# The first modulation share: half of its sums on TensorE, between the transposes of x

## The chip, the cores and the metric

The kernel runs on one core of a Trainium2 chip. The metric is the device time of one launch in microseconds (us). The engines are TensorE (PE; PEld is its weight load), VectorE (DVE), ScalarE (ACT), GpSimd (POOL) and SyncE (SP), which here only issues transfers.

## The reference, cut to what matters

One transformer block over 512 tokens of 1024 features, all in fp32. What the change touches is the very start, where a condition vector `c` is turned into a shift and a scale for every feature and these are applied to the normalized input:

```
cond = jax.nn.silu(c)
mod = (cond @ ada_w[l] + ada_b[l]).reshape(B, 6, D_MODEL)[:, :, None, :]
shift1, scale1, gate1 = mod[:, 0], mod[:, 1], mod[:, 2]
u = rmsnorm(x, norm_mix[l]) * (1.0 + scale1) + shift1
aq, ak, av, bq, bkv, biq, bik, biw, cq, ck, cv, g = split_cols(u @ w_in[l])
```

Everything behind it (three attention branches, gates, output projection, a feed-forward layer and a last norm) is left as it is.

## The kernel before, in words

Every product of the block needs `u`, and `u` needs two things: the normalized x with features on partitions (`xnT`), and the shift and the scale of each feature (`ab`).

**x.** Four tiles of 128 tokens by 1024 features (512 KB each) are fetched into `xt`. For tile t, ACT squares and sums it (`x_square`, L317) and takes the root (L320), DVE takes the reciprocal (L321) and multiplies the tile by it (L322), TensorE turns it in eight 128x128 transposes into two PSUM tiles `xtp` (`x_turn`, L328), and `x_copy` (L336 on DVE, L338 on ACT) copies the two halves into `xnT`. The loop at L409 runs these steps of several tiles interleaved.

**The modulation shares.** shift1 and scale1 are `cond @ ada_w` over 1024 rows. The 1024 features are cut into four shares of 256 features. For share q, `fetch_share(q)` fetches eight row blocks k of 128 rows (256 KB each: 256 columns of the shift and 256 of the scale) into `ada`, and then three 256 KB slices of the first weights (`raw_b` twice, `raw_bq`). `mod_sums` multiplies every row block by its column of `cond` and adds up the blocks in two accumulators `gsum`: the first two blocks as a scaled copy on ACT (L356), the other six as multiply-and-add on DVE (L358), then the two accumulators are added (L360). What is left, a sum over the 128 partitions, is done by TensorE in `mod_columns` (L368): for each 128 features one matmul of the `gsum` block (as weights) with a column of ones, four of them in a share. DVE then adds the bias and makes `ab` (L371, L373), ACT makes `uh` (L377) out of `xnT` and `ab`, and TensorE's real work starts with `p_kv` (L448). From there the products of share q run while ACT and DVE make the sums of share q+1.

**The bias table.** Two small matmuls `tps` (L431) and two ACT copies `ts` (L432) make a table that the attention reads much later. They stand behind the loop over x.

**What sets the order.** The schedule is written out by hand: each engine runs its instructions in the order of the program text and waits in place. SP issues the transfers in program order as well. `warm(n)` (L457) issues n matmuls of the identity that nobody reads, 7 ahead of `mod_columns(0)` and 5 behind it.

Of the kernel before, what the change touches and what calls it, by code (L numbers as in the profile page):

```python
# [13 lines left out]
F32 = mybir.dt.float32  # L14
F32R = mybir.dt.float32r
AF = mybir.ActivationFunctionType
# [4 lines left out]
S = 512  # L21
D = 1024
NT = 4
KT = 8
# [95 lines left out]
def block_kernel(ctx: ExitStack, tc: tile.TileContext, x, c, rel_bias, ada_w, ada_b, norm_mix, w_in,  # L120
                 gate_b, diff_lambda, diff_subln, dsa_kv_norm, dsa_w_uv, w_br_a, w_br_b, w_br_c, w_o,
                 norm_mlp, w_ff1, w_ff2, norm_final, onehot, out):
    nc = tc.nc
    x, out = x[0], out[0]
# [9 lines left out]
    dram = ctx.enter_context(tc.tile_pool(name="dram", bufs=1, space=bass.MemoryType.DRAM))  # L134
# [5 lines left out]
    def bank(tag, name):  # L140
        return ps.tile([128, 512], F32, tag=tag, name=name, bufs=banks[tag])

    def big_tile(name, dt=F32, shape=(128, 8, 512)):
        return big.tile(list(shape), dt, tag="big", name=name)
# [8 lines left out]
    def rows(w, r0, nk, c0, n):  # L153
        return w[r0:r0 + nk * 128, c0:c0 + n].rearrange("(k p) c -> p k c", p=128)
# [105 lines left out]
    rb = const.tile([33, 12], F32, name="rb")  # L260
# [8 lines left out]
    start = ExitStack()  # L269
    st = start.enter_context(tc.tile_pool(name="st", bufs=1))  # L270
    oh = st.tile([33, 640], F32, name="oh")
    nc.gpsimd.dma_start(oh, onehot)
    xt = big_tile("xt", shape=(128, 4, 1024))
    for t in range(NT):
        nc.sync.dma_start(xt[:, t], x[t * 128:(t + 1) * 128])
    for r0, src, n in small_rows:
        nc.gpsimd.dma_start(vrow[r0:r0 + n], src.rearrange("o (r p) -> (o r) p", p=128))

# [2 lines left out]
    SHARES = ((0, 2), (2, 4), (4, 6), (6, 8))  # L281
    ada = {}
    for n in QS:
        pool, tag = (st, "") if n == "b1" else (wp, "raw")
        raws[n] = pool.tile([128, 8, 256], F32, tag=tag or "raw1", name=f"raw_{n}")

    def fetch_share(q):
        k0, k1 = SHARES[q]
        n, c0 = (k1 - k0) * 128, k0 * 128
        ada[q] = st.tile([128, 8, 2, 256], F32, tag="ada", name=f"ada{q}", bufs=2)[:, :, :, 0:n]  # L290
        if n == 128:
            for g in range(2):
                for sl in range(2):
                    nc.sync.dma_start(ada[q][:, 4 * g:4 * g + 4, sl, :], rows(ada_w, g * 512, 4, sl * 1024 + c0, n))
        else:
            for k in range(KT):
                nc.sync.dma_start(ada[q][:, k], ada_w[k * 128:(k + 1) * 128, 0:2048].rearrange(
                    "p (s c) -> p s c", s=2)[:, :, c0:c0 + n])
        for name in QS:
            nc.sync.dma_start(raws[name][:, k0:k1], chunks[name][0][:, k0:k1])  # L300

    for q in range(2):
        fetch_share(q)
# [3 lines left out]
    cond = const.tile([128, 8], F32, name="cond")  # L307
# [8 lines left out]
    def x_square(t):  # L316
        nc.scalar.activation(junk, xt[:, t], AF.Square, accum_out=xss[t])  # L317

    def x_norm(t):
        nc.scalar.activation(xss[t], xss[t], AF.Sqrt, bias=eps, scale=1.0 / D)  # L320
        nc.vector.reciprocal(xss[t], xss[t])  # L321
        nc.vector.tensor_scalar(xt[:, t], xt[:, t], xss[t], None, op0=ALU.mult)  # L322

    def x_turn(t):
        for g in range(2):
            tp = xtp[t, g] = bank(("S", "O")[g], f"xtp{t}{g}")
            for k in range(4):
                nc.tensor.transpose(tp[:, k * 128:(k + 1) * 128],  # L328
                                    xt[:, t, (4 * g + k) * 128:(4 * g + k + 1) * 128], ident)

    def x_copy(t):
        for g in range(2):
            dst = xnT[:, 4 * g:4 * g + 4, t * 128:(t + 1) * 128]
            srcv = xtp[t, g].rearrange("p (k q) -> p k q", k=4)
            if g == 0 and t < 2:
                nc.vector.tensor_copy(dst, srcv)  # L336
            else:
                nc.scalar.activation(dst, srcv, AF.Copy)  # L338
# [8 lines left out]
    def mod_sums(q, ks):  # L347

        n = 128 * (SHARES[q][1] - SHARES[q][0])
        if 0 in ks:  # L350
            gsum[q] = [st.tile([128, 2, 256], F32, tag=f"gsum{i}", name=f"gsum{q}{i}", bufs=2)[:, :, 0:n]
                       for i in range(2)]
        for k in ks:
            acc, src = gsum[q][k % 2], ada[q][:, k]
            if k < 2:
                nc.scalar.activation(acc, src, AF.Copy, scale=cond[:, k:k + 1])  # L356
            else:
                nc.vector.scalar_tensor_tensor(acc, src, cond[:, k:k + 1], acc, op0=ALU.mult, op1=ALU.add)  # L358
        if KT - 1 in ks:
            nc.vector.tensor_tensor(gsum[q][0], gsum[q][0], gsum[q][1], op=ALU.add)  # L360

    def mod_columns(q):
        k0, k1 = SHARES[q]
        nk = k1 - k0
        gps = bank("S", f"gps{q}")
        for s in range(2):
            for k in range(nk):
                nc.tensor.matmul(gps[:, s * nk + k:s * nk + k + 1], gsum[q][0][:, s, k * 128:(k + 1) * 128], ones,  # L368
                                 start=True, stop=True)
        ks = slice(k0, k1)  # L370
        nc.vector.tensor_tensor(ab[:, :, ks], gps[:, 0:2 * nk].rearrange("p (s k) -> p s k", s=2), vmod[:, :, ks],  # L371
                                op=ALU.add)
        nc.vector.scalar_tensor_tensor(ab[:, 1, ks], ab[:, 1, ks], 1.0, vcol[:, C_NM + k0:C_NM + k1],  # L373
                                       op0=ALU.add, op1=ALU.mult)
# [31 lines left out]
    nc.vector.tensor_scalar(cond, cond, 1.0, None, op0=ALU.add)  # L406
    nc.vector.reciprocal(cond, cond)
    nc.vector.tensor_tensor(cond, cond, cps[:, 0:8], op=ALU.mult)
    for t in range(NT + 2):  # L409
        if t < NT:  # L410
            x_square(t)
            x_norm(t)
        if t == NT - 1:
            mod_sums(0, (0, 1))
        if t > 1:
            x_copy(t - 2)
        if t == NT:
            vps = bank("T", "vps")
            nc.tensor.transpose(vps[:, 0:C_ALL], vrow, ident[0:C_ALL, 0:C_ALL])
            nc.scalar.activation(vcol, vps[:, 0:C_ALL], AF.Copy)  # L420
        if 0 < t <= NT:
            x_turn(t - 1)
    mod_sums(0, range(2, KT))


    tab = dram.tile([12, 640], F32, name="tab")
    tabw = [dram.tile([4, 128, 640], F32, name=f"tabw{g}") for g in range(3)]
    ts = st.tile([12, 640], F32, name="ts")
    for a, b, tag in ((0, 512, "S"), (512, 640, "T")):
        tps = bank(tag, f"tps{a}")  # L430
        nc.tensor.matmul(tps[0:12, 0:b - a], rb, oh[:, a:b], start=True, stop=True)  # L431
        nc.scalar.activation(ts[:, a:b], tps[0:12, 0:b - a], AF.Copy)  # L432
    nc.gpsimd.dma_start(tab, ts)

    first = {n: bank(tag, f"p_{n}") for n, tag in (("kv", "mm"), ("iq0", "mm"), ("iq1", "S"), ("ik", "S"),
                                                   ("bq00", "O"), ("bq01", "O"))}

# [16 lines left out]
    def warm(n):  # L454

        for _ in range(n):
            nc.tensor.matmul(warm_ps[:, 0:128], ident, ident, start=True, stop=True)  # L457

    LAST = len(SHARES) - 1
    warm(7)  # L460
    mod_columns(0)
    warm(5)
    split_share(0, QS[:1])
    make_uh(0)
    split_share(0, QS[1:])
    make_ul(0)
    mod_sums(1, range(4))

    def first_two(q):
# [3 lines left out]
    for q in range(LAST):  # L473
        if q + 2 <= LAST:
            fetch_share(q + 2)
        mod_sums(q + 1, range(4, KT))
        rest = b_part(2, q)
        for _ in chain(first_two(q), islice(rest, 4)):
            pass
        split_share(q + 1, QS[:1])  # L480
        if q + 2 <= LAST:
            mod_sums(q + 2, (0, 1))
        mod_columns(q + 1)
        make_uh(q + 1)
        if q + 2 <= LAST:
            mod_sums(q + 2, (2, 3))
        split_share(q + 1, QS[1:])
        make_ul(q + 1)
        if q + 1 == LAST:
            fetch(3)  # L490
            fetch(4)
        for _ in rest:
            pass
# [706 lines left out]
    tns, tps = {}, {}  # L1200
# [381 lines left out]
```

## Time and profile before

| | |
|---|---|
| three runs | 844.58, 839.05, 843.79 us, median 843.79 us |
| the profiled execution | 841.24 us, its span (first to last instruction) 839.5 us |
| mean granted clock of TensorE in it | 0.995 |
| TensorE busy | 808.7 us (96%) |
| VectorE busy | 570.8 us (68%) |
| ScalarE busy | 411.7 us (49%) |
| moved by DMA | 116.48 MB, mean 139 GB/s |

The page of the profile gives busy time by engine and the span in 40 slices; TensorE is at 0.8 or more in every slice but the first (0.5) and the last (0.6). So the program is one long row of TensorE work, and its start is the only stretch where TensorE has little to do for long. The timeline lists an engine's instructions in order, neighbours of one kind merged: start, duration until the last of them ends, engine, line, operation, tiles and count, and in brackets how long the engine had been idle and what released it.

### The profile page before, as it was taken

To read this page: it belongs to the slowest core of one execution; us is meant where nothing else is said; L and a number is where in the kernel's file an instruction comes from. 1 tells how busy PE (TensorE), PEld (TensorE's weight loads), DVE (VectorE), ACT (ScalarE), POOL (GpSimd) and SP (SyncE) were. 2 spreads that over 40 slices of the span, in tenths; PEclk is the share of its full clock that TensorE was granted. 3 is DMA by queue.
4 is the path that set the end of the run, shared out by engine and by line. 5 is a ranking of instruction groups with operands and counts; after the bars stand their busy time and mean duration, and the time that the engine had idled before them with its cause. 6 is when DMAs were issued, how large, how long until landed. Compare 5 with 4: busy or idle time off the path is not lost. (4 is left out here: it accounts for less than half of the span.)

```text
span 839.5 us, 10498 instructions
## 1 busy us (share of the span) xinstructions
PE 808.7 (96%) x3865; PEld 644.8 (77%) x3865; DVE 570.8 (68%) x992; ACT 411.7 (49%) x712; POOL 186.9 (22%) x130
## 2 busy tenths in 40 slices
PE   5899999999999999899999989999999999999996
PEld 4778867678777776557787879888888888888885
DVE  5866785678878359885445685874678567857554
ACT  7655634552434365345652446554553356335433
POOL 2014322202562224552247370000000000010020
PEclk9999999999999999999999999999999999999998
DMA  9946451133656376512135528113511441172202
GB/s 308 347 136 207 172 195 66 51 100 110 196 194 215 95 264 189 164 35 92 50 101 197 206 68 322 60 51 114 188 50 51 162 140 50 51 248 102 99 4 100
DMA packets 81535, 116.48 MB, mean 139 GB/s; under 512 B 4590, under 2 KB 53274, under 8 KB 81484
## 3 DMA queue, kind: packets, MB, share of 16 engines
q1 hardware_dynamic: 78812, 107.73, 39.0%
q0 software_dynamic: 2672, 8.09, 2.7%
q8 instruction: 30, 0.49, 0.2%
q14 instruction: 21, 0.17, 0.1%
HBM read 110.25 MB, written 8.17 MB: 141 GB/s over the span
## 5 line engine op out<-in xcount | busy, mean ns | idle before, releaser
L1266 PE MATMUL pf<-u2h,hi_f 128*128 128x512 f32 x224 | 87.1, 389 | 0.0
L1268 PE MATMUL pf<-u2l,hi_f 128*128 128x512 f32 x224 | 87.1, 389 | 0.0
L1270 PE MATMUL pf<-u2h,lo_f 128*128 128x512 f32 x224 | 87.1, 389 | 0.0
L947 DVE SCALAR_TENSOR_TENSOR adacc<-adch,cond,adacc 128x512 f32<-128x512 f32 x56 | 61.5, 1098 | 3.9 <-DMA adch<-in_ada_w_dram 3.4
L236 DVE TENSOR_TENSOR lo_f<-raw_f,hi_f 128x1024 fp32r<-128x1024 f32 x38 | 46.6, 1255 | 16.9 <-ACT hi_f L224 16.9
L1436 POOL DMA_DIRECT2D x1f<-x1d x4 | 2.1, 537 | 234.3 <-PE pp L1412 234.3
L224 ACT ACTIVATE hi_p<-w 128x1024 fp32r<-128x1024 f32 x36 | 36.3, 1050 | 34.0 <-PE pp L1412 27.1
L236 DVE TENSOR_TENSOR lo_p<-w,hi_p 128x1024 fp32r<-128x1024 f32 x36 | 42.7, 1221 | 9.8 <-ACT hi_p L224 9.8
L224 ACT ACTIVATE hi_f<-raw_f 128x1024 fp32r<-128x1024 f32 x38 | 38.6, 1048 | 21.5 <-PE p2l L1528 7.1
L1270 PEld LDWEIGHTS pf<-u2h,lo_f 128*128 128x128 f32 x224 | 42.0, 188 | 8.7
L1266 PEld LDWEIGHTS pf<-u2h,hi_f 128*128 128x128 f32 x224 | 42.0, 188 | 8.7
L1268 PEld LDWEIGHTS pf<-u2l,hi_f 128*128 128x128 f32 x224 | 42.0, 188 | 8.7
L1412 PE MATMUL pp<-hi_p,hq 128*128 128x512 f32 x144 | 45.8, 389 | 0.0
L236 POOL TENSOR_TENSOR lo_gb<-raw_gb,hi_gb 128x1024 fp32r<-128x1024 f32 x8 | 20.0, 2519 | 65.3 <-ACT hi_gb L224 65.3
L1412 PEld LDWEIGHTS pp<-hi_p,hq 128*128 128x128 f32 x144 | 27.0, 188 | 5.6
L726 ACT ACTIVATE Pa<-Pa,nma 128x128 f32<-128x128 f32 (+3 forms) x32 | 17.7, 554 | 27.7 <-DVE nma L722 27.6
L1412 PE MATMUL pp<-hi_p,he 128*128 128x512 f32 x96 | 30.5, 389 | 0.0
L1412 PE MATMUL pp<-hi_p,ha 128*128 128x512 f32 x96 | 30.5, 389 | 0.0
L1406 DVE TENSOR_TENSOR acc<-acc,pp 128x512 f32<-128x512 f32 x32 | 21.7, 683 | 10.6 <-PE pp L1412 10.6
L236 POOL TENSOR_TENSOR lo_gc<-raw_gc,hi_gc 128x1024 fp32r<-128x1024 f32 x8 | 19.2, 2413 | 41.7 <-ACT hi_gc L224 41.7
L1412 PE MATMUL pp<-lo_p,hq 128*128 128x512 f32 x72 | 28.1, 390 | 0.0
L527 PE MATMUL p_gb<-uh,hi_gb 128*128 128x512 f32 x64 | 27.5, 430 | 0.0
(429 smaller groups left out, 2329.2 us busy)
## 6 DMA issues: line engine op xcount, KB each, us to landing
raw_f<-in_w_ff_dram SPq DMA_DIRECT2D x20, 1024.0 KB
adch<-in_ada_w_dram SPq DMA_DIRECT2D x64, 256.0 KB
w<-in_w_ff_dram SPq DMA_DIRECT2D x12, 1024.0 KB
ada<-in_ada_w_dram SPq DMA_DIRECT2D x32, 256.0 KB
raw_gc<-in_w_in_dram SPq DMA_DIRECT2D x4, 1024.0 KB
raw_gb<-in_w_in_dram SPq DMA_DIRECT2D x4, 1024.0 KB
raw_a<-in_w_in_dram SPq DMA_DIRECT2D x4, 1024.0 KB
raw_ga<-in_w_in_dram SPq DMA_DIRECT2D x4, 1024.0 KB
```

The costliest lines, as they stand in the source:

```text
L224: nc.scalar.activation(parts[n][0][:, sl], raws[n][:, sl], AF.Copy)
L236: eng.tensor_tensor(parts[n][1][:, sl], raws[n][:, sl], parts[n][0][:, sl].bitcast(F32), op=ALU.subtract)
L527: nc.tensor.matmul(dst, wh[:, k, cs], uh[:, k], start=k == 0, stop=False)
L726: nc.scalar.activation(p[:, 0:w], p[:, 0:w], AF.Exp, bias=nm, scale=-1.0, accum_out=sm)
L947: nc.vector.scalar_tensor_tensor(acc, ach[n], cond[:, k:k + 1], acc, op0=ALU.mult, op1=ALU.add)
L1266: nc.tensor.matmul(dst, wh[:, i, cs], u2h[:, i], start=i == 0, stop=False)
L1268: nc.tensor.matmul(dst, wh[:, i, cs], u2l[:, i], start=False, stop=False)
L1270: nc.tensor.matmul(dst, wl[:, i, cs], u2h[:, i], start=False, stop=i == KT - 1)
L1406: nc.vector.tensor_tensor(c, c, dst[t], op=op)
L1412: nc.tensor.matmul(dst[t], a[:, part, k, j, ts_], w[:, k], start=not onto and k == 0 and m == 0, stop=k == 3 and m == 2, skip_group_check= ...
L1436: nc.gpsimd.dma_start(x1f[:, t], x1d[t * 128:(t + 1) * 128])
```

## The change

In `mod_sums` of share 0 only the row blocks 4 to 7 are left: blocks 4 and 5 are the scaled copies on ACT, blocks 6 and 7 the multiply-and-adds on DVE. Blocks 0 to 3 go to TensorE (`mod_rows`): for each block four matmuls, the `ada` block as weights and the column of `cond` as the one moving column, adding up in the PSUM tile `gps0`. They stand in two pairs of blocks, behind the transposes of x tile 0 and of x tile 2. `mod_columns(0)` adds its four columns onto the same tile. The transfers alternate: x tiles 0 and 1, ada blocks 0 and 1, x tile 2, ada blocks 2 and 3, x tile 3, ada blocks 4 to 7. The bias table moves into the loop, behind the transposes of x tile 1. All four first halves of `x_copy` are on DVE now (before: of tiles 0 and 1). The seven `warm` matmuls ahead of `mod_columns(0)` are gone. Shares 1 to 3 are left as they were.

```diff
     xt = big_tile("xt", shape=(128, 4, 1024))
-    for t in range(NT):
-        nc.sync.dma_start(xt[:, t], x[t * 128:(t + 1) * 128])
...
+    def fetch_x(t):
+        nc.sync.dma_start(xt[:, t], x[t * 128:(t + 1) * 128])
+
     def fetch_share(q):
...
+        if q == 0:
+            fetch_x(0)
+            fetch_x(1)
...
             for k in range(KT):
                 nc.sync.dma_start(ada[q][:, k], ada_w[k * 128:(k + 1) * 128, 0:2048].rearrange(
                     "p (s c) -> p s c", s=2)[:, :, c0:c0 + n])
+                if q == 0 and k in (1, 3):
+                    fetch_x(2 + k // 2)
...
-            if g == 0 and t < 2:
+            if g == 0:
                 nc.vector.tensor_copy(dst, srcv)
...
-        if 0 in ks:
+        k0 = 0 if q else PE_ROWS
+        if k0 in ks:
...
-            if k < 2:
+            if k < k0 + 2:
                 nc.scalar.activation(acc, src, AF.Copy, scale=cond[:, k:k + 1])
...
+    PE_ROWS = 4
+    gps0 = bank("S", "gps0")
+
+    def mod_rows(ks):
+        nk = SHARES[0][1] - SHARES[0][0]
+        for k in ks:
+            for s in range(2):
+                for j in range(nk):
+                    nc.tensor.matmul(gps0[:, s * nk + j:s * nk + j + 1], ada[0][:, k, s, j * 128:(j + 1) * 128],
+                                     cond[:, k:k + 1], start=k == 0 and s == 0 and j == 0, stop=False, skip_group_check=True)
...
-        gps = bank("S", f"gps{q}")
+        gps = bank("S", f"gps{q}") if q else gps0
...
+    def bias_table():
+        for a, b, tag in ((0, 512, "S"), (512, 640, "T")):
+            tps = bank(tag, f"tps{a}")
+            nc.tensor.matmul(tps[0:12, 0:b - a], rb, oh[:, a:b], start=True, stop=True)
+            nc.scalar.activation(ts[:, a:b], tps[0:12, 0:b - a], AF.Copy)
+        nc.gpsimd.dma_start(tab, ts)
+
     for t in range(NT + 2):
         if t < NT:
             x_square(t)
             x_norm(t)
         if t == NT - 1:
-            mod_sums(0, (0, 1))
+            mod_sums(0, (4, 5))
         if t > 1:
             x_copy(t - 2)
...
         if 0 < t <= NT:
             x_turn(t - 1)
-    mod_sums(0, range(2, KT))
...
+        if t in (1, 3):
+            mod_rows((t - 1, t))
+        if t == 2:
+            bias_table()
+        if t == NT:
+            mod_sums(0, (6, 7))
...
-    warm(7)
     mod_columns(0)
     warm(5)
```

TensorE at its start, before; each x tile gives two rows of `xtp`, `x4` is a count of matmuls:

```order
L328 MATMUL xtp_161<-ident,xt 128x128 x4
L328 MATMUL xtp_166<-ident,xt 128x128 x4
L328 MATMUL xtp_177<-ident,xt 128x128 x4
L328 MATMUL xtp_182<-ident,xt 128x128 x4
L328 MATMUL xtp_197<-ident,xt 128x128 x4
L328 MATMUL xtp_202<-ident,xt 128x128 x4
L419 MATMUL vps<-ident,vrow 128x82
L328 MATMUL xtp_212<-ident,xt 128x128 x4
L328 MATMUL xtp_217<-ident,xt 128x128 x4
L431 MATMUL tps_236<-oh,rb 12x512
L431 MATMUL tps_239<-oh,rb 12x128
L457 MATMUL warm<-ident 128x128 x7
```

The same place in the change; `gps_146` is `gps0`, and its matmuls out of `ada_107` are `mod_rows`:

```order
L334 MATMUL xtp_167<-ident,xt 128x128 x4
L334 MATMUL xtp_172<-ident,xt 128x128 x4
L378 MATMUL gps_146<-cond,ada_107 128x1 x8
L334 MATMUL xtp_191<-ident,xt 128x128 x4
L334 MATMUL xtp_196<-ident,xt 128x128 x4
L437 MATMUL tps_201<-oh,rb 12x512
L437 MATMUL tps_204<-oh,rb 12x128
L334 MATMUL xtp_218<-ident,xt 128x128 x4
L334 MATMUL xtp_223<-ident,xt 128x128 x4
L378 MATMUL gps_146<-cond,ada_107 128x1 x8
L451 MATMUL vps<-ident,vrow 128x82
L334 MATMUL xtp_241<-ident,xt 128x128 x4
```

Eight one-column matmuls stand between the transposes of tile 0 and tile 1, and the bias table's two matmuls behind those of tile 1.

ScalarE from the square of x tile 2 on (`ss_141`) to the two scaled copies, before:

```order
L317 ACTIVATE junk,ss_141<-xt 128x1024
L320 ACTIVATE ss_141<-ss_141,eps 128x1
L338 ACTIVATE xnT<-xtp_166 128x4x128
L317 ACTIVATE junk,ss_142<-xt 128x1024
L320 ACTIVATE ss_142<-ss_142,eps 128x1
L356 ACTIVATE gsum_191<-ada_109,cond 128x512
L356 ACTIVATE gsum_192<-ada_109,cond 128x512
```

And in the change:

```order
L323 ACTIVATE junk,ss_141<-xt 128x1024
L326 ACTIVATE ss_141<-ss_141,eps 128x1
L344 ACTIVATE xnT<-xtp_172 128x4x128
L438 ACTIVATE ts<-tps_201 12x512
L438 ACTIVATE ts<-tps_204 12x128
L323 ACTIVATE junk,ss_142<-xt 128x1024
L326 ACTIVATE ss_142<-ss_142,eps 128x1
L363 ACTIVATE gsum_212<-ada_107,cond 128x512
L363 ACTIVATE gsum_213<-ada_107,cond 128x512
```

The two copies `ts` of the bias table stand ahead of the square of x tile 3 (`ss_142`) now; before, they stood at the end of the loop, behind the last copy of `xnT`.

## Rows read from the trace of the kernel before

**Rows 1.** The page, busy us and share of the span by engine.
```profile
PE 808.7 (96%) x3865; PEld 644.8 (77%) x3865; DVE 570.8 (68%) x992; ACT 411.7 (49%) x712; POOL 186.9 (22%) x130
```

**Rows 2.** Windows: length, busy us by engine, granted clock, DMA share, GB/s.
```profile
10.00:15.00 5.00, 4.32 (x23) 2.91 (x23) 4.32 (x9) 4.97 (x12) 0.00 (x0) 1.00 1.10 349
...
45.00:50.00 5.00, 4.64 (x26) 3.70 (x24) 4.48 (x7) 0.33 (x1) 0.00 (x0) 1.00 0.00 0
```

**Rows 3.** Timeline of SP's transfer issues: start, until the last issue, tiles, count.
```profile
1.21 1.78 SPq L275 DMA_DIRECT2D xt<-in_x_dram  x4
...
8.80 0.37 SPq L297 DMA_DIRECT2D ada<-in_ada_w_dram  x1
...
10.41 0.37 SPq L297 DMA_DIRECT2D ada<-in_ada_w_dram  x1
...
10.96 1.12 SPq L300 DMA_DIRECT2D raw_b<-in_w_in_dram  x2
...
13.23 5.64 SPq L297 DMA_DIRECT2D ada<-in_ada_w_dram  x8
```

**Rows 4.** Timeline of TensorE, the start and the first sums of share 1.
```profile
7.18 3.67 PE L328 MATMUL xtp<-ident,xt 128*128 128x128 f32 x16 [4.44 <-DVE xt L322]
...
14.47 1.24 PE L431 MATMUL tps<-oh,rb 33*12 33x512 f32 x4
...
18.55 1.02 PE L368 MATMUL gps<-ones,gsum 128*128 128x1 f32 x8 [0.19 <-DVE gsum L360]
...
21.00 0.50 PE L448 MATMUL p_kv<-uh,hi_b 128*128 128x512 f32 x1 [0.20 <-ACT uh L377]
...
29.70 1.02 PE L368 MATMUL gps<-ones,gsum 128*128 128x1 f32 x8 [1.79 <-DVE gsum L360]
```

**Rows 5.** L328 in 7.1 to 12.2 us, then in 13.1 to 14.6: ns min/median/max.
```profile
L328 PE MATMUL xtp<-ident,xt x20: 421/421/475, 7.2 to 12.0; 128*128 128x128 f32 x20
...
L328 PE MATMUL xtp<-ident,xt x8: 272/273/329, 13.2 to 14.3; 128*128 128x128 f32 x8
```

**Rows 6.** Timeline of ScalarE.
```profile
8.80 1.06 ACT L317 ACTIVATE junk<-xt 128x1024 f32<-128x1024 f32 x1 [1.10 <-DMA xt<-in_x_dram]
...
10.66 1.05 ACT L317 ACTIVATE junk<-xt 128x1024 f32<-128x1024 f32 x1
...
15.76 0.72 ACT L432 ACTIVATE ts<-tps 12x512 f32<-12x512 f32 x2
16.99 0.63 ACT L399 ACTIVATE hi_b<-raw_b 128x512 fp32r<-128x512 f32 x1 [0.51 <-DMA raw_b<-in_w_in_dram]
20.14 1.52 ACT L377 ACTIVATE uh<-xnT,ab 128x512 fp32r<-128x512 f32 x2 [2.51 <-DVE ab L373]
```

**Rows 7.** Timeline of VectorE, share 0 and then share 1.
```profile
12.36 0.75 DVE L322 TENSOR_SCALAR xt<-xt,ss 128x1024 f32<-128x1024 f32 x1
13.03 0.68 DVE L336 COPY xnT<-xtp 128x512 f32<-128x512 f32 x1
13.63 4.06 DVE L358 SCALAR_TENSOR_TENSOR gsum<-ada,cond,gsum 128x512 f32<-128x512 f32 x6
17.72 0.69 DVE L360 TENSOR_TENSOR gsum<-gsum,gsum 128x512 f32<-128x512 f32 x1
...
24.76 4.06 DVE L358 SCALAR_TENSOR_TENSOR gsum<-ada,cond,gsum 128x512 f32<-128x512 f32 x6
...
28.86 0.69 DVE L360 TENSOR_TENSOR gsum<-gsum,gsum 128x512 f32<-128x512 f32 x1
```

**Rows 8.** Windows around 118 us, columns as in the other windows.
```profile
116.00:118.00 2.00, 0.15 (x3) 0.11 (x2) 1.82 (x4) 0.72 (x3) 1.69 (x1) 1.00 0.26 105
...
118.30:121.60 3.30, 3.30 (x10) 1.81 (x9) 2.29 (x13) 0.66 (x3) 0.00 (x0) 0.50 0.96 330
```

**Rows 9.** Waits of TensorE over the span: total us, times, longest us.
```profile
PE tpa L732 <- DVE Pa L1083: 3.6, 3, 1.9
...
PE u2p L1238 <- POOL tn L1233: 2.4, 2, 1.6
```

More of the change, by code (lines that the diff above doesn't have):

```diff
@@ L368, in mod_columns @@
                 nc.tensor.matmul(gps[:, s * nk + k:s * nk + k + 1], gsum[q][0][:, s, k * 128:(k + 1) * 128], ones,
-                                 start=True, stop=True)
+                                 start=q > 0, stop=True, skip_group_check=True)
         ks = slice(k0, k1)
@@ L408, in block_kernel @@
     nc.vector.tensor_tensor(cond, cond, cps[:, 0:8], op=ALU.mult)
+    tab = dram.tile([12, 640], F32, name="tab")
+    tabw = [dram.tile([4, 128, 640], F32, name=f"tabw{g}") for g in range(3)]
+    ts = st.tile([12, 640], F32, name="ts")
+    def bias_table():
[4 more added lines that the diff above has]
+        nc.gpsimd.dma_start(tab, ts)
     for t in range(NT + 2):
@@ L422, in block_kernel @@
             x_turn(t - 1)
-    mod_sums(0, range(2, KT))
[L426 to L433, printed above, removed]
+        if t in (1, 3):
[4 more added lines that the diff above has]
+            mod_sums(0, (6, 7))
     first = {n: bank(tag, f"p_{n}") for n, tag in (("kv", "mm"), ("iq0", "mm"), ("iq1", "S"), ("ik", "S"),
```

## The prediction

> **What bounds the kernel now.** I read the page first: TensorE is busy for 808.7 us of the 839.5 us span [rows 1], so a time is gained or lost only where TensorE stands still, or where all of its later work is pushed. Then the timeline of the first 32 us, engine by engine, with the windows beside it. TensorE's row of real work begins with `p_kv` at 21.00 us [rows 4]. From there it is pushed along as a whole: its later waits are for VectorE, ScalarE or GpSimd chains that start from the same work [rows 9], so they move with it. The question is when `p_kv` starts, and whether share 1 follows.
>
> Read backwards, `p_kv` waits for `uh` on ScalarE, which waited 2.51 us for `ab` [rows 6]. `ab` follows the four `gps` matmuls at 18.55, and these were released by the last sum on VectorE [rows 4], which ran 17.72 to 18.41 [rows 7]. Ahead of it VectorE worked without a gap from 12.36: the multiply of x tile 3, one copy, six multiply-and-adds. That chain began when ScalarE had squared tile 3 and taken its root. So x tile 3 starts the chain that ends in `p_kv`: square at 10.66 [rows 6], multiply at 12.36, last sum ending at 18.41 [rows 7], `p_kv` at 21.00.
>
> Share 1 hangs on the same chain: VectorE starts its six sums at 24.76 and closes them at 28.86 without a wait for data [rows 7], and TensorE stands 1.79 us for that [rows 4]. Its last ada block had landed by about 24.6 (below), so what limits share 1 is VectorE's row of work behind `ab` of share 0. A shift of `ab` arrives there undiminished, up or down, and later shares follow.
>
> The transfers run at the limit from the start: DMA share 1.10 and 349 GB/s in 10 to 15 us, nothing left in 45 to 50 [rows 2]. SP keeps eight transfers under way: the seventh ada block was issued at 8.80, the moment at which ScalarE's wait for x tile 2 ended, eight transfers earlier [rows 3, 6]. So an issue dates a landing: x tile 3 landed by 10.41, ada block 0 by 10.96, block 3 by 13.23 [rows 3]. The eight issues from 13.23 are (5.64 - 0.37)/7 = 0.75 us apart, the price of 256 KB. Share 1's eight blocks therefore land from about 19.2 to 24.5.
>
> **The change part by part.** All terms are against these times.
>
> *Transfers.* No byte is added; the order changes. x tile 3 now stands behind ada blocks 0 to 3, so it lands when these bytes had all landed before: 13.2 instead of 10.4, 2.8 us later. Blocks 0 and 1 come where tile 2 was, by about 8.8; tile 2 where tile 3 was, by 10.4. Blocks 4 to 7 and the weights land as before.
>
> *Sums taken off VectorE.* Four multiply-and-adds of (17.72 - 13.63)/6 = 0.68 us go, 2.73 us. One more `x_copy` comes ahead of the sums: 13.63 - 13.03 = 0.60. From the start of the multiply of tile 3 to the end of the last sum it was 18.41 - 12.36 = 6.05; it becomes 6.05 - 2.73 + 0.60 = 3.92. That is the gain, 2.13 us, if that multiply starts as early as it did.
>
> *One-column matmuls on TensorE.* Sixteen, in two groups of eight; the trace shows the same form in `gps`: four of them are 8 instructions in 1.02 us, about (1.02 - 0.25)/7 = 0.11 us each [rows 4]. Eight are 16 instructions: 1.8 us at that pace. But the first group stands right behind the transposes of tile 0, and up to 12.2 us a transpose took 421 ns where after 13.1 it took 273 [rows 5]; 16 transposes were (3.67 - 0.42)/15 = 0.217 us apart [rows 4]. The window prints a granted clock of 1.00 there [rows 2], but the paces say the 1.2 GHz level before, 2.4 after, with the change near 12.3, some 5 us after the first transpose. At half pace the group costs 16 x 0.22 = 3.5 us. Bounds: 1.8 and 3.5; I take 3.5, since the group runs at 8.9 to 12.4, where the slow rows stand.
>
> *What queues behind it.* Transposes of tile 0 from 7.18, eight at 0.217: to 8.9. The group: to 12.4 (its blocks have landed). Transposes of tile 1, at the fast pace, 0.9: to 13.3. Before, they were through by 10.85. Then the bias table's matmuls `tps`, 1.24: first half ready 1.0 after its start, at 14.4. Now the copies `ts` on ScalarE, 0.72 [rows 6]: 14.4 to 15.15. And behind these, in ScalarE's order, is the square of x tile 3. So it starts at about 15.1, not at 13.2 when its data are there, and not at 10.66: 4.4 us later. This is the step on which the forecast rests: a table that nobody needs early has been put ahead of the first link of the chain, on an engine that waits in place for TensorE.
>
> *From there.* Square to multiply is 12.36 - 10.66 = 1.70, so the multiply starts at 16.8 and the last sum ends at 16.8 + 3.92 = 20.7, against 18.41: 2.3 us later. ScalarE's two scaled copies end near 17.9, before VectorE asks for them at 18.7. `ab`, `uh` and `p_kv` follow at the old distance, 21.00 - 18.41 = 2.59: `p_kv` at 23.3. `hi_b` ended at 17.6 before [rows 6] and will end near 20, under the same wait. The second group of one-column matmuls (about 15.4 to 17.2, fast) and the transposes of tile 3 (to about 18.4) are done before the last sum, so they cost nothing. The missing `warm` matmuls save nothing: TensorE was waiting there.
>
> *Sum:* -2.13 (VectorE) + 4.4 (start of tile 3) = +2.3 us. On the profiled execution's own 841.24 us that is 843.5. That execution lies 2.6 under the median of the three runs, 843.79; the mean of all four is 842.2, which I take as the base: **844.5 us**.
>
> **A rule weighed against a row.** Rows 5 show that transposes alone brought TensorE from the half to the full pace: but for one tiny transpose at the start nothing else had run. The Trainium skill, TensorE: Matmul & The Clock Gate, section Part 4: PE-mode transpose, says that the full clock does not engage for transposes. By that rule the pace would still have been half at 13 us; this trace disagrees. It is kept as the late-clock rival below, since the new one-column matmuls might do as little for the clock.
>
> **The rivals.**
>
> *Early data path (+0.4).* If the clock rises by about 10 us, or the columns cost less than taken, the copies `ts` are through at 13.2 and tile 3's landing alone decides: multiply at 14.9, last sum at 18.8, +0.4: 842.6. For it: the rise came 5 us after the first transpose with a gap between; against: it would have to be two microseconds earlier.
>
> *Late clock (+4.3).* If the pace stays half until 15 us, the transposes of tile 1 cost 0.85 more and `tps` some 1.1 more: +4.3, 846.5. For it, TensorE's new work is thin; against, rows 5.
>
> *A half-clock stretch later (+4.0).* In 116 to 118 us TensorE had next to nothing to do, and the next 3.3 us ran at a granted clock of 0.50 [rows 8]. The change leaves TensorE idle from about 18.4 to 20.85 ahead of `gps`, where seven `warm` matmuls stood. If the clock falls there, some 3.4 us at half pace cost 1.7 on top of 2.3: 846.2. Against: the 1.79 us wait at 27.9 [rows 4] had no such sequel. [...]
>
> *The gain arrives (-0.8), the other side.* If ScalarE squares tile 3 before 12.8 us, the shorter VectorE chain wins; break-even is a multiply at 18.41 - 3.92 = 14.5. The most it can give is set by ada block 7, which lands 0.75 ahead of `raw_b` (16.99, rows 6), at 16.2: last sum by 17.6, 0.8 earlier: 841.4. For it: VectorE's load is really smaller; against: tile 3 would have to land before bytes that now stand ahead of it, and `ts` would have to be early.
>
> **How the numbers follow.** Forecast 0.48, early data 0.15, late clock 0.12, half-clock stretch 0.13, gain 0.12. By themselves the cases span 841.4 to 846.5. The runs before lie from 839.05 to 844.58, so a median can be off by two or three: range **840 to 849**. All cases are within 1% of the time before (8.4 us), which is about what a measurement of this kernel can tell from no change: within 1% 0.94; faster by over 1% 0.02, slower by over 1% 0.04, for a second stall that none of the cases holds.
>
> **What would show it.** In the profile after: x tile 3's square at about 15.1, waiting for `ts` (a wait of `ts` for `tps` of some 2 us on ScalarE); the first `mod_rows` group 3.5 us long; VectorE's two sums at about 18.7 and 19.3; `p_kv` at 23.3; share 1's `gps` about 2.3 later than 29.70. A square of tile 3 at 13.2 with an idle release by its DMA would show the early rival; `p_kv` before 21 the gain; a granted clock of 0.50 behind 21 us the half-clock stretch. The forecast is wrong if `ts` isn't late, or if share 1 takes up the shift.

## The result, and the profile after

Twenty runs of each kernel: 846.84 us median with the change (845.16 to 848.42), 841.25 before (839.05 to 844.58). The ratio is 1.0062, 95% interval 1.0052 to 1.0071: **slower by 5.6 us between the medians, 0.6% by the ratio**. That is within 1%, inside the range of 840 to 849, and on the side that was forecast, but more than twice the 2.3 us of the sum. The profiled execution has a span of 845.2 us against 839.5. The page of the change:

```profile
PE 817.2 (97%) x3883; PEld 653.6 (77%) x3883; DVE 569.5 (67%) x990; ACT 410.5 (49%) x710; POOL 186.8 (22%) x130
```

TensorE is busy for 8.5 us more [rows 1], and the added matmuls are few (18 instructions more in all). The timeline of TensorE after the change, to set beside [rows 4]:

```profile
7.10 1.97 PE L334 MATMUL xtp<-ident,xt 128*128 128x128 f32 x8 [4.58 <-DVE xt L328]
8.86 3.41 PE L378 MATMUL gps<-cond,ada 128*128 128x1 f32 x16
12.13 1.95 PE L334 MATMUL xtp<-ident,xt 128*128 128x128 f32 x8
14.01 2.31 PE L437 MATMUL tps<-oh,rb 33*12 33x512 f32 x4
16.57 1.97 PE L334 MATMUL xtp<-ident,xt 128*128 128x128 f32 x8 [0.25 <-ACT ts L438]
18.33 3.41 PE L378 MATMUL gps<-cond,ada 128*128 128x1 f32 x16
...
21.77 1.91 PE L334 MATMUL xtp<-ident,xt 128*128 128x128 f32 x8
23.48 1.71 PE L387 MATMUL gps<-ones,gsum 128*128 128x1 f32 x8
...
27.18 0.77 PE L474 MATMUL p_kv<-uh,hi_b 128*128 128x512 f32 x1
...
35.25 1.02 PE L387 MATMUL gps<-ones,gsum 128*128 128x1 f32 x8 [0.60 <-DVE gsum L367]
```

Every row up to 25 us has the slow pace: the second group of one-column matmuls takes 3.41 us like the first, `tps` 2.31 instead of 1.24, the four columns of `mod_columns` 1.71 instead of 1.02, and the last transposes as long as the first. TensorE hardly waits any more; it is late by itself. The same in the durations (ns min/median/max) of the transposes, and of the first products:

```profile
L334 PE MATMUL xtp<-ident,xt x32: 421/421/476, 7.1 to 23.3; 128*128 128x128 f32 x32
...
L474 PE MATMUL p_kv<-uh,hi_b x2: 628/701/774, 27.2 to 28.2; 128*128 128x512 f32 x2
...
L474 PE MATMUL p_kv<-uh,lo_b x1: 397/397/397, 29.0 to 29.0; 128*128 128x512 f32 x1
```

All 32 transposes take 421 ns; before, it was 421 up to 12 us and 273 after 13 [rows 5]. Only at about 29 us does a 512-column matmul reach the 0.4 us that it had before from 21 us on. So the array ran at its 1.2 GHz level for 16 us longer. (The clock column of the windows prints 1.00 up to the first rise in both traces, so the paces have to be read, not that column.) ScalarE and VectorE in the change, the links of the chain that the prediction followed:

```profile
9.82 1.06 ACT L323 ACTIVATE junk<-xt 128x1024 f32<-128x1024 f32 x1 [2.40 <-DMA xt<-in_x_dram]
...
15.93 0.74 ACT L438 ACTIVATE ts<-tps 12x512 f32<-12x512 f32 x2 [4.14 <-PE tps L437]
16.58 1.04 ACT L323 ACTIVATE junk<-xt 128x1024 f32<-128x1024 f32 x1
```

```profile
18.27 0.75 DVE L328 TENSOR_SCALAR xt<-xt,ss 128x1024 f32<-128x1024 f32 x1
...
20.14 1.41 DVE L365 SCALAR_TENSOR_TENSOR gsum<-ada,cond,gsum 128x512 f32<-128x512 f32 x2
21.57 0.69 DVE L367 TENSOR_TENSOR gsum<-gsum,gsum 128x512 f32<-128x512 f32 x1
...
25.29 0.16 DVE L390 TENSOR_TENSOR ab<-gps,vcol 128x4 f32<-128x4 f32 x1 [1.73 <-PE gps L387]
```

The same `ab` before:

```profile
19.68 0.16 DVE L371 TENSOR_TENSOR ab<-gps,vcol 128x4 f32<-128x4 f32 x1 [1.28 <-PE gps L368]
```

The mechanism of the forecast is there: ScalarE waits 4.14 us for `tps`, and the square of x tile 3 follows `ts` at 16.58 (15.1 was forecast). VectorE's shorter sums end at 22.26 (20.7). But then `ab` comes 3.0 us behind the last sum, where it came 1.3 behind it before [rows 7], because TensorE is still turning tile 3 (until 23.7) and `mod_columns` is slow too. `p_kv` starts 6.2 us later, the `gps` of share 1 5.55 later (35.25 against 29.70, rows 4), and the span is 5.7 longer: what is lost by share 1 is carried to the end.

### The profile page after: what moved, and what is told of

Its sections match the earlier page's. It is cut to its first block, busy times and chain, and to the rows that moved or that the text cites. A ratio compares the mean times of both kernels' runs of the same rounds, so it can differ in the third digit from the quotient of the medians.

```text
span 845.2 us, 10526 instructions
## 1 busy us (share of the span) xinstructions
PE 817.2 (97%) x3883; PEld 653.6 (77%) x3883; DVE 569.5 (67%) x990; ACT 410.5 (49%) x710; POOL 186.8 (22%) x130
```

## The experiments

Two theories. **Late clock**: the one-column matmuls between the first transposes go with a TensorE that stays at its half pace, and that is a large part of the loss. **The order alone**: the table's copies ahead of x tile 3, and the added matmuls, cost the 5.6 us at whatever pace. The ratios are of run times, to runs of the kernel before on the same chip; the two columns of times are from the one profiled execution of each kernel.

| run | what it is | ratio to before (95%) | `p_kv` at, us | `gps` of share 1 at |
| --- | --- | --- | --- | --- |
| before | the kernel before | 1 | 21.00 | 29.70 |
| the change | all of it | 1.0062 (1.0052 to 1.0071) | 27.18 | 35.25 |
| e1_early_warm | the change, TensorE warmed first | 1.0029 (1.0016 to 1.0042) | 26.40 | 34.55 |
| e2_table_back | the change, table behind the loop | 1.0026 (1.0008 to 1.0045) | 24.59 | 32.66 |
| e3_cols | before, unread one-column matmuls added | 1.0073 (1.0048 to 1.0098) | 29.32 | 38.01 |
| e4_turns | before, unread transposes added | 1.0014 (0.9999 to 1.0029) | 22.01 | 30.70 |
| e5_no_rows | the change without `mod_rows` | 1.0034 (1.0017 to 1.0051) | 25.81 | 33.88 |
| e7_wide | the change, 128 columns in `mod_rows` | 1.0028 (1.0011 to 1.0044) | 23.68 | 32.38 |
| e8_wide_back | e7_wide, table behind the loop | 0.9993 (0.9977 to 1.0010) | 21.96 | 30.57 |
| v1_late_rows | before, last two blocks on TensorE, 128 columns | 0.9978 (0.9959 to 0.9997) | 20.70 | 29.41 |
| v1_narrow | v1_late_rows with one column | 0.9985 (0.9969 to 1.0000) | 19.77 | 28.46 |
| v2_late_table | v1_late_rows, table moved into share 1 | 1.0016 (1.0000 to 1.0032) | 19.83 | 29.50 |

**Is it the one-column matmuls?** Two kernels add work that nobody reads to the kernel before, in the two places where the change has `mod_rows`: once 16 one-column matmuls, once 32 transposes. Both are 32 instructions.

```
+    fill_ps = bank("mm", "fill")
+    def fill(n):                                   # e3_cols
+        for i in range(n):
+            nc.tensor.matmul(fill_ps[:, 0:1], ident, cond[:, 0:1], start=True, stop=True)
+    def fill(n):                                   # e4_turns
+        for i in range(2 * n):
+            nc.tensor.transpose(fill_ps[:, 0:128], ident, ident)
...
         if 0 < t <= NT:
             x_turn(t - 1)
+        if t in (1, 3):
+            fill(8)
```

> The kernel before, with sixteen matmuls of the identity with one column of cond (32 instructions, their sums read by nobody) added in the two places where the change has its own: behind the transposes of x tiles 0 and 2. Theory 'late clock' (with these matmuls between the transposes the clock rises late): transposes at 421 ns well behind 13 us, the granted clock first recorded well behind 12.4 us, p_kv behind 26, time 846 or more. Rival (the lateness comes from the change's transfers and moved table, which leave TensorE in other waits): the clock rises at 12 to 13 as before, the added matmuls cost 3.5 + 1.8 us of TensorE's slack, p_kv at about 22.5, time about 842.5.

> As the run with one-column matmuls in the kernel before, but with 32 transposes of the identity (32 instructions too, of 128 columns each) in their places, so that TensorE is taken for about as long. Theory 'late clock' in its narrow form (it is the one-column matmuls, not the time they take): the clock rises at 12 to 13 us as in the kernel before, p_kv at about 22.5, time about 842.5. Rival (anything that pushes the transposes of x does it): as late as the run with one-column matmuls, 846 or more.

With one-column matmuls the time is 6.1 us higher, with transposes 1.2. The transposes of x in the first, the whole start:

```profile
L328 PE MATMUL xtp<-ident,xt x32: 421/421/475, 7.1 to 20.5; 128*128 128x128 f32 x32
```

and its table right behind them (1.24 before, rows 4):

```profile
20.84 2.30 PE L440 MATMUL tps<-oh,rb 33*12 33x512 f32 x4
```

The transposes of x in the second, 7 to 12 and 12 to 17 us:

```profile
L328 PE MATMUL xtp<-ident,xt x12: 272/421/476, 7.0 to 11.9; 128*128 128x128 f32 x12
...
L328 PE MATMUL xtp<-ident,xt x22: 270/272/273, 11.8 to 15.9; 128*128 128x128 f32 x22
```

In both, TensorE is taken without a gap from 7 us until its table is through, by the same number of instructions, and no transfer, table or sum differs from before. With transposes the pace doubles by 12 us; with one-column matmuls it is still the slow one at 23. So the added form alone makes the clock late here. The added work costs 1.2 us at the early clock, so some 4.9 of the 6.1 are the late clock's: nearly what the whole change loses.

**Does that hold in the change itself?** The same sums with 128 moving columns instead of one:

```
+    condx = st.tile([128, 136], F32, name="condx")          # zeros, cond in its first 8 columns
...
-                    nc.tensor.matmul(gps0[:, s * nk + j:s * nk + j + 1], ada[0][:, k, s, j * 128:(j + 1) * 128],
-                                     cond[:, k:k + 1], ...)
+                    nc.tensor.matmul(gps0[:, (s * nk + j) * 128:(s * nk + j + 1) * 128],
+                                     ada[0][:, k, s, j * 128:(j + 1) * 128], condx[:, k:k + 128], ...)
```

> The change, with one thing else: each of the sixteen mod_rows matmuls streams 128 columns instead of one (the column of cond, and behind it columns that nobody reads; the tile for them costs one small copy on VectorE). Same weights, same number of instructions. Theory 'late clock by the one-column matmuls': the clock rises at 11 to 13 us, transposes of x tile 1 at 273 ns, the first group of mod_rows still about 3.5 us and the second 1.8; then the working of the prediction holds with its own numbers: the copies ts end near 15.1, x tile 3 is squared there, p_kv at about 23.3, time about 2.3 above before, 844. Rival (the transfers and the moved table make the clock late, whatever the columns): p_kv near 27, 847.

The transposes of x behind the first group, then TensorE's and ScalarE's timeline of this kernel:

```profile
L336 PE MATMUL xtp<-ident,xt x24: 272/273/329, 11.6 to 19.4; 128*128 128x128 f32 x24
```

```profile
13.80 1.24 PE L441 MATMUL tps<-oh,rb 33*12 33x512 f32 x4 [1.17 <-DVE xnT L344]
...
16.44 1.95 PE L380 MATMUL gps<-condx,ada 128*128 128x128 f32 x16
...
23.68 0.50 PE L478 MATMUL p_kv<-uh,hi_b 128*128 128x512 f32 x1
...
32.38 1.02 PE L390 MATMUL gps<-ones,gsum 128*128 128x1 f32 x8 [1.72 <-DVE gsum L369]
```

```profile
14.87 0.74 ACT L442 ACTIVATE ts<-tps 12x512 f32<-12x512 f32 x2 [2.21 <-PE tps L441]
15.52 1.04 ACT L325 ACTIVATE junk<-xt 128x1024 f32<-128x1024 f32 x1
```

The clock is up by 11.6 us. 128 columns cost hardly more than one (at the fast pace 16 instructions take 1.95 us here, and 1.84 with one column in e1_early_warm and e2_table_back). And now the prediction's sum comes out: tile 3 squared at 15.5 (15.1 forecast), `p_kv` at 23.7 (23.3), share 1 2.7 us later, the time 2.4 above before (2.3). One link was reached by another way, though: the first group and the transposes of tile 1 were through at 12.6 (13.3 forecast), and then `tps` waited 1.17 us for VectorE's copy into `xnT`, a wait that the prediction did not have. That the sum fits to the tenth is in part luck. One column instead of 128 is worth the other half of the loss.

**And the table?** It is moved back behind the loop over x, once in the change as it is and once with the wide matmuls:

```
-        if t == 2:
-            bias_table()
         if t == NT:
             mod_sums(0, (6, 7))
+    bias_table()
```

> The change, with the bias table (two matmuls, two copies, one store) moved back behind the loop over x. Theory 'late clock': x tile 3 is squared at about 12.5 instead of 16.6, but the transposes and the second group of one-column matmuls still run at the half pace up to about 21, so the last sums wait for TensorE and not for VectorE; p_kv at about 25, time about 845, less than half of the loss given back. Rival 'the order alone', in the form of the prediction (the table's copies push x tile 3 by 4.4 us and all else follows): p_kv below 22.5 and the time at 842 or less.

> The last one, and the bias table moved back behind the loop over x: both suspects mended at once. If the two explain the loss, x tile 3 is squared when it lands (13.2 to 13.9), the last sum ends at 18.9 to 19.6 as the data path alone gives, p_kv at about 21.5 to 22.2, and the time is 0.5 to 1.2 above before, 842. If something else is at work (the alternating transfers cost more than the 2.8 us of x tile 3), it stays above 844.

The run with one column is at 1.0026: 3 us of 5.2 given back (both by the ratios), where "less than half" was expected of the one theory and nearly all of it of the other. Its TensorE shows why neither fits whole:

```profile
16.27 1.84 PE L378 MATMUL gps<-cond,ada 128*128 128x1 f32 x16
...
24.59 0.77 PE L473 MATMUL p_kv<-uh,hi_b 128*128 128x512 f32 x1
```

```profile
19.70:26.40 6.70, 6.70 (x25) 5.47 (x24) 2.70 (x6) 4.62 (x10) 0.51 (x1) 0.50 1.09 350
```

The clock was up by 16.3 us, behind two tiles of transposes in a row, and down again (0.50, half) from 19.7 on, after the second one-column group. Its ten executions are of two kinds: six took 841.9 to 844.3 us with a mean granted clock of 0.991 to 0.993, and four took 845.0 to 846.7 us, nearly as long as the change, with 0.995 to 0.998. The clock column prints 1.00 up to the first rise, so a high mean with a long time fits a first rise as late as in the change; but the profiled execution is of the faster kind, and this is not shown.

With both mended (wide, table back) the loss is gone: 0.9993, with ScalarE and TensorE where the data path alone would have them:

```profile
13.77 1.06 ACT L325 ACTIVATE junk<-xt 128x1024 f32<-128x1024 f32 x1 [0.67 <-DMA xt<-in_x_dram]
```

```profile
21.96 0.79 PE L477 MATMUL p_kv<-uh,hi_b 128*128 128x512 f32 x1
...
30.57 1.05 PE L390 MATMUL gps<-ones,gsum 128*128 128x1 f32 x8 [0.40 <-DVE gsum L369]
```

```profile
22.00:25.00 3.00, 3.00 (x7) 2.38 (x8) 1.84 (x3) 3.00 (x6) 0.00 (x0) 0.50 1.09 355
```

Share 1 is 0.9 us late here (30.57 against 29.70): x tile 3 is squared 3.1 later than before, and VectorE's shorter sums give 2.1 of that back. The window shows the granted clock at 0.50 behind `p_kv` in this kernel too, without any one-column matmul in `mod_rows`. So the four kernels make a table of two times two. By the `gps` of share 1: 5.55 late with both parts, 2.96 without the table's move, 2.68 without the narrow form, 0.87 without either. By these single executions the table's move is worth 1.8 to 2.6 us and the narrow form 2.1 to 2.9. By the ratios of the run times each is worth about 0.35%, 2.9 us, whether the other is there or not: the two add up.

**The rest of the change without `mod_rows`:** `PE_ROWS = 0`, and all eight blocks summed on ScalarE and VectorE.

> The change without its mod_rows: all sums of share 0 on ScalarE and VectorE as before, but the alternating transfers, the table in the loop, the copies of x on VectorE and the missing warm matmuls stay. Theory 'late clock by the one-column matmuls': with only transposes at the start the clock rises at 11 to 13 us; the order alone then costs: x tile 3 squared at about 14.6, the last of six sums at about 22.9, p_kv at about 25.5, time about 845.5. Rival: the clock is as late as in the change (behind 25 us) and the time 847 or more.

2.9 us above before; TensorE and VectorE:

```profile
10.44 1.24 PE L437 MATMUL tps<-oh,rb 33*12 33x512 f32 x4
13.90 1.97 PE L334 MATMUL xtp<-ident,xt 128*128 128x128 f32 x8 [2.21 <-DVE xnT L342]
...
21.95 1.87 PE L387 MATMUL gps<-ones,gsum 128*128 128x1 f32 x8 [4.36 <-DVE gsum L367]
```

```profile
17.11 4.06 DVE L365 SCALAR_TENSOR_TENSOR gsum<-ada,cond,gsum 128x512 f32<-128x512 f32 x6
```

Without one-column matmuls ahead of it the clock is up by 10.4 us (`tps` in 1.24), as expected. That `p_kv` is at 25.8 (25.5) is luck: the last sum ended at 21.9, 1.0 earlier than expected, but in the wait of 4.36 us the granted clock fell to 0.50 (20.5 to 27.3 us), `gps` took 1.87, and `p_kv` came 3.9 behind the last sum instead of 2.6. Tile 3 was squared at 13.5, as it landed: the copies `ts`, in the same place as in the change, were through at 13.4. So the table's place did harm only where something held up its matmuls: the slow work ahead of them in the change, the wait for VectorE's copy in e7_wide. The six sums start at 17.1 instead of 13.6 [rows 7], so x tile 3's later place costs as such. `mod_rows` does relieve VectorE: with 128 columns `p_kv` comes 2.1 earlier than here (23.68); with one column the late clock takes more than that back.

**Warming TensorE before the first tile** (two identity matmuls ahead of `cps`, ten behind it, while nothing else is there):

> The change, with twelve matmuls of the identity more on TensorE while it has nothing to do (two ahead of the first small transpose, ten behind it, until about 7 us). Theory 'late clock' (the first 29 us of the change run at the half pace, and that is most of its loss): a transpose of x tile 0 or 1 takes about 273 ns instead of 421, the first group of one-column matmuls 1.8 us instead of 3.4, the bias table's copies are through at 12.7, p_kv starts at about 20.7 instead of 27.2, and the time falls to about 841, level with the kernel before. Rival 'the order alone' (the table's copies ahead of x tile 3 and the added matmuls cost the 5.6 us whatever the clock): p_kv stays behind 24 and the time above 844.

The rival's numbers came (`p_kv` at 26.40, 844.75 us), but they don't speak for its reason, because the half pace was not removed. The clock was up for the first group (16 one-column instructions in 1.84 us), and then fell:

```profile
8.00 1.84 PE L378 MATMUL gps<-cond,ada 128*128 128x1 f32 x16
...
13.23 2.31 PE L445 MATMUL tps<-oh,rb 33*12 33x512 f32 x4 [2.46 <-DVE xnT L342]
```

```profile
13.00:30.00 17.00, 16.52 (x64) 13.84 (x65) 8.94 (x17) 10.72 (x20) 0.51 (x1) 0.50 1.09 350
```

Being early, TensorE ran into a wait of 2.46 us for a PSUM tile that VectorE had not yet copied out, and from 13 to 30 us the granted clock was 0.50, the 1.2 GHz level, over the second group too. Whether the wait or the one-column group brought it down can't be told from this run. In e5_no_rows the clock fell to 0.50 in a wait of 2.21 us for the same copy as well (13.6 us), with no one-column matmul ahead of it; but there 16 transposes followed and it was up again at 17.0, while here, with the second one-column group between them, it stayed down until 30. So a warm start does not last through this order.

**Versions from what was learnt.** The order of before, but the last two row blocks on TensorE, in place of the seven `warm` matmuls; 128 columns in the one, one column in the other:

```
-    warm(7)
+    mod_rows((6, 7))
     mod_columns(0)
```

> A version made from what was learnt: the kernel before, with its own order of transfers and its table where it was, but the last two row blocks (6 and 7, the last to land) are summed by TensorE, 128 columns wide, between the table and mod_columns, in place of the seven warm matmuls; VectorE sums blocks 2 to 5. Block 7 lands at 16.2; TensorE is done with both blocks at 17.4, VectorE's last sum ends at 17.0 instead of 18.4, mod_columns ends at 18.3 instead of 19.6, p_kv at 19.6 instead of 21.0: about 1.4 us below before, 839.8. If share 1 does not follow (its sums wait for data), the gain is lost there and the time stays at 841.

> The version with the last two row blocks on TensorE and the table in its old place, but its mod_rows matmuls stream one column as in the change. They stand behind all transposes of x, when the clock has risen (12.4 us before, 14.9 in the last run). If one-column matmuls do harm only where they stand between the first transposes, the clock rises as early, p_kv is at about 20.7 and the time is that of the wide version, 0.9 to 1.8 below before. If they bring the clock down again wherever they stand, a granted clock of 0.50 is seen within the next 10 us and the time is level with before or above.

Both are a little faster than before, 0.9978 and 0.9985, though their intervals end at or near 1. The wide one:

```profile
15.26 1.24 PE L449 MATMUL tps<-oh,rb 33*12 33x512 f32 x4
...
20.70 0.50 PE L466 MATMUL p_kv<-uh,hi_b 128*128 128x512 f32 x1 [0.21 <-ACT uh L394]
```

The expected 19.6 for `p_kv` was missed by 1.1: `tps` stood ahead of the row blocks, and ended at 16.5. In the narrow one `tps` started at 14.33, nearly a microsecond earlier, though its program is the same up to there but for one small copy and a memset on VectorE; so the 0.9 between the two at `p_kv` (20.70 and 19.77) are no price of the 128 columns. In the narrow one the granted clock fell at `p_kv`:

```profile
15.51 1.95 PE L372 MATMUL gps<-cond,ada 128*128 128x1 f32 x16
...
19.77 0.80 PE L463 MATMUL p_kv<-uh,hi_b 128*128 128x512 f32 x1
...
28.46 1.02 PE L383 MATMUL gps<-ones,gsum 128*128 128x1 f32 x8 [0.68 <-DVE gsum L362]
```

```profile
19.40:22.60 3.20, 3.11 (x9) 2.21 (x8) 1.65 (x4) 3.20 (x6) 0.00 (x0) 0.50 1.09 354
```

This is the granted clock of 0.50 that its second theory named, but it does not show that theory: in e8_wide_back it fell around `p_kv` too, with 128 columns. And the time is the one of its first: TensorE would have waited for VectorE's sums of share 1 anyway, and its wait there only shrank to 0.68 us, where it was 1.79 [rows 4]. From `p_kv` to the `gps` of share 1 it is 8.69 us here and 8.70 before, so this half-paced stretch cost nothing. Last, the table moved into that wait (`bias_table()` ahead of `mod_columns(1)`):

> The version with the last two row blocks on TensorE, and the bias table moved to where TensorE waits for the sums of share 1 (27.7 to 29.4 us in the last run). There the table's matmuls stood from 15.26 to 16.5 ahead of the row blocks, which had landed by then, so mod_columns ended at 19.3. Without them the row blocks start at about 15.5 and mod_columns ends at about 18.5: p_kv at 19.9 instead of 20.7, share 1's gps at about 28.9, time another 0.5 to 0.8 lower, 1.7 to 2.5 below before. If the table's copies on ScalarE hold up share 1's gps instead (its PSUM tile is the one they read), share 1 starts as late as in the last run and the gain is lost there.

```profile
19.83 0.50 PE L468 MATMUL p_kv<-uh,hi_b 128*128 128x512 f32 x1 [0.21 <-ACT uh L394]
...
29.50 1.05 PE L385 MATMUL gps<-ones,gsum 128*128 128x1 f32 x8 [1.50 <-ACT ts L452]
```

```profile
31.20:34.50 3.30, 3.30 (x9) 2.60 (x8) 2.86 (x5) 3.30 (x6) 0.00 (x0) 0.50 1.09 353
```

`p_kv` came at 19.8 as worked out, and the gain was lost as its rival said: the `gps` of share 1 waited 1.50 us for the copies `ts`, which stood behind scaled copies that waited for data. The medians are 1.5 us apart on the slow side (842.68 against 841.15), and the rival doesn't account for that, since share 1 was still 0.2 ahead of before. In the profiled execution a half-paced stretch followed (the window above), and share 2's `gps` was 1.0 late (40.41 against 39.38); whether the other executions had it too is open.

## Why the prediction was right or wrong

*What bounds the kernel.* Right. `p_kv`, and through VectorE share 1, set the time; 5.55 us at share 1 became 5.7 at the end.

*Transfers.* Right in size: in the three kernels where ScalarE waited for its landing (e2_table_back, e5_no_rows, e8_wide_back) x tile 3 was squared at 13.5 to 13.9; 13.2 had been worked out. Tile 2 was squared at 9.82 in the change and at 10.7 to 11.3 in these and in e7_wide, with the same order of transfers (10.4 worked out), so the same landing came over a microsecond apart from one execution to the next.

*VectorE's sums.* Right: from tile 3's multiply to the end of the last sum 22.26 - 18.27 = 3.99, forecast 3.92.

*The table's copies ahead of tile 3.* Right as a mechanism, and e7_wide gives the forecast's sum nearly to the tenth (+2.4), one link of it by another way: the wait of 1.17 us for VectorE's copy, a term that the prediction put at nothing. Moving the table back is worth 2 to 3 us, with one column and with 128.

*The pace of TensorE.* This step failed: the change of pace "near 12.3, some 5 us after the first transpose", with everything behind the first group "at the fast pace". The group itself was priced right (3.41 us, forecast 3.5). But the rise was taken over from the kernel before as if it were bound to the time since the first transpose. With the one-column group in these microseconds it came at about 29 here and behind 23 in e3_cols. The steps named as costing nothing (the second group, tile 3's transposes, the removed `warm`, the distance of 2.59 from the last sum to `p_kv`) were each priced at the fast pace. At the slow one the transposes of tile 1 and `tps` brought tile 3's square 1.5 us later than forecast (16.58), and behind the last sum the transposes of tile 3 and `mod_columns` stood on the path: that distance became 27.18 - 22.26 = 4.9, 2.3 longer. With the forecast 2.3 and 0.1 in the chain between, this makes up the 6.2 at `p_kv`.

*The number.* The range of 840 to 849 held, but its width came from the spread of the runs before. The forecast time, 844.5, is only 2.3 below the measured median because the base taken, 842.2, was 0.9 above the 841.25 of the twenty runs; the loss itself was 3.3 too small. That part is luck.

*The rivals.* The late-clock rival was the case that came, and it had 0.12, and 4.3 us where 5.6 were measured, because it let the clock rise at 15 us and so priced nothing behind the last sum. Against it rows 5 were put, which show that transposes bring the clock up; they say nothing of one-column matmuls, which the kernel before never had among its first instructions. The gain of 0.8 did not come; the early data path (+0.4) is near what e8_wide_back shows at share 1 (+0.9), but only with the table moved back. A half-clock stretch ahead of `gps` could not come in the change, where the clock had not risen yet; e7_wide waited 1.55 us there without one, e5_no_rows 4.36 us with one.

*The rule on transposes.* The Trainium skill, TensorE: Matmul & The Clock Gate, section Part 4: PE-mode transpose, says that the full clock does not engage for transposes. The runs go against it a second time: with 32 more transposes the transposes of x reached 272 ns by 12 us. The forecast rightly followed the row. What went with a late clock in these runs were the one-column groups (421 ns transposes until 23.3 us in the change and 20.5 in e3_cols); the prediction named that case in its late-clock rival and gave it too small a chance.

## What to carry to other kernels

Before work is moved onto an idle TensorE at the start of a kernel, ask at which pace it will run there, and what brings the pace up: a duration read behind the rise must not be used ahead of it, and the moment of the rise must not be taken over when other instructions stand ahead of it. Making the one-column matmuls 128 columns wide cost about 0.1 us for 16 instructions here; ahead of the rise it was worth 2 to 3 us, behind it (v1_late_rows against v1_narrow) no gain shows. And on an engine that waits in place, a piece of work that nobody needs early does harm ahead of the first link of a chain as soon as its own input is late, even inside a stretch that looks idle: in e5_no_rows the table's copies stood there and cost nothing, in the change and e7_wide they held up tile 3.

## What the runs showed of the hardware that was not expected

Besides the late rise: **a half-paced stretch behind a short wait was there in some profiled executions and absent in another, at a place where the program is the same.** At the first `tpc` TensorE waited 1.85 to 1.86 us for VectorE in the three executions compared here. In the kernel before and in the change a stretch of 3.3 us at a granted clock of 0.50 began within 1.1 us of the end of that wait ([rows 8], and here the change):

```profile
124.60:127.90 3.30, 3.30 (x10) 2.13 (x10) 2.08 (x8) 0.30 (x3) 0.00 (x0) 0.50 0.98 331
```

In the profiled execution of v1_late_rows the same wait is followed by the full clock:

```profile
118.00:121.40 3.40, 3.40 (x18) 2.27 (x17) 2.79 (x13) 1.29 (x5) 0.00 (x0) 1.00 0.96 326
```

Its lead over the kernel before is 0.17 us at this `tpc` (117.75 against 117.92) and 1.69 at the next one (121.03 against 122.72), so the stretch cost the kernel before 1.5 us. That is nearly all of the 1.7 by which the spans differ (837.8 against 839.5). The same happened at the `gps` of share 1: before, 1.79 us of waiting had no sequel [rows 4]; in e4_turns a wait of 1.80 us at that place was followed by 0.50 from 31.4 us on. What decides whether the stretch comes was not tried. Each kernel here was profiled once, so a difference of one or two microseconds between two spans, or at a marker behind such a stretch, need not come from the edit; the ratios of many runs, and the shift of a marker ahead of any stretch, are the better measures.
